# Average pooling by four on one core: input and result buffers resized, all transfers on one queue

## The chip, the cores and the metric

The kernel runs on one core of a Trainium2 chip. The metric is the device time of a whole execution in microseconds. Lower is better. The kernel before takes 1555.81 us, the median of 3 runs from 1555.76 to 1555.83.

## The reference

The input `x` is float32 of shape (64, 256, 8192), the kernel size and the stride are 4. Every group of four neighbours along the last axis becomes its mean:

```python
for i in range(out_len):            # out_len = 2048
    start = i * stride
    output[:, :, i] = np.mean(x[:, :, start : start + kernel_size], axis=2)
```

Because 8192 is a multiple of four and the groups do not overlap, the input can be read as one flat array of 134,217,728 numbers, and the output is a flat array of a quarter of that. 536.87 MB are read and 134.22 MB written.

## The kernel before

The flat array is cut into blocks. A block takes 128 x `w` numbers that lie in one piece in memory; each of the 128 partitions gets `w` of them in a row. There are 63 blocks with `w` = `FULL` = 16384 (64 KB per partition, 8.39 MB), and then a tail of five smaller ones, 8192, 4096, 2048, 1280 and 768 wide. The five tail blocks share one input tile and one result tile, each in a slice of its own.

There are two input buffers of 64 KB per partition (`xin`) and four result buffers of 16 KB (`res`). For each block three functions are called:

- `load` (the DMA is line 62) takes an input buffer and issues the load on SP's queue. Two blocks are loaded ahead; once the first tail block's turn comes, all of the tail is. A load into a buffer that was used before waits, on SP, until the second addition has read that buffer's earlier block.
- `means` adds on VectorE (DVE): line 71 adds even to odd elements in place in the input buffer, line 72 adds the neighbours of that result into the result tile. ScalarE (ACT) multiplies by a quarter in place (line 80). For the last block VectorE does this (line 76).
- `store` (line 85) issues the store of the result. Nearly all stores are issued on ACT's queue; the last full block's and the first tail block's are on SP's.

Each engine executes its instructions in the order in which the program issues them, and waits where an operand or a buffer is not ready. SP's and ACT's DMAs stand in the profile as two queues, q1 and q10. Every DMA between 128 partitions and memory is spread over the core's 16 DMA engines, eight partitions each. In the records of the trace, one partition's row is one packet, and a small packet ends each engine's share of a DMA.

Of the kernel before, what the change touches and what calls it, by code (L numbers as in the profile page):

```python
# [1 line left out]

# [4 lines left out]


FULL = 16384
BUFS_IN = 2  # L10
BUFS_OUT = 4

HEAD = ()
TAIL = (8192, 4096, 2048, 1280, 768)


@with_exitstack
def kernel(
    ctx: ExitStack,
    tc: tile.TileContext,  # L20
    x: bass.AP,
    kernel_size: bass.AP,
    stride: bass.AP,
    out: bass.AP,
):
    nc = tc.nc
    K, S = int(kernel_size), int(stride)
    assert K == S == 4
    B, C, L = x.shape
    assert L % K == 0  # L30
    P = nc.NUM_PARTITIONS
    dt = x.dtype
    add = mybir.AluOpType.add


    xf = x.rearrange("b c l -> (b c l)")
    of = out.rearrange("b c l -> (b c l)")
    rest = B * C * L // P - sum(HEAD) - sum(TAIL)
    assert rest % FULL == 0
    blocks = [(w, i == 0) for i, w in enumerate(HEAD)]  # L40
    blocks += [(FULL, True)] * (rest // FULL)
    blocks += [(w, i == 0) for i, w in enumerate(TAIL)]
    n = len(blocks)
    first = n - len(TAIL)

    pin = ctx.enter_context(tc.tile_pool(name="xin", bufs=BUFS_IN))
    pout = ctx.enter_context(tc.tile_pool(name="res", bufs=BUFS_OUT))

    xs, begins = {}, [0]
    for w, _ in blocks:  # L50
        begins.append(begins[-1] + w)

    def load(i):

        w, fresh = blocks[i]
        if fresh:
            load.tile, load.at = pin.tile([P, FULL], dt, name="xt"), 0
        a = load.at
        load.at += w
        src = xf[P * begins[i] : P * begins[i + 1]].rearrange("(p m) -> p m", p=P)  # L60
        xs[i] = load.tile[:, a : a + w]
        nc.sync.dma_start(out=xs[i], in_=src)  # L62

    def means(i):
        w, fresh = blocks[i]
        if fresh:
            means.tile, means.at = pout.tile([P, FULL // K], dt, name="ot"), 0
        a = means.at
        means.at += w // K
        o, xt = means.tile[:, a : a + w // K], xs.pop(i)  # L70
        nc.vector.tensor_tensor(out=xt[:, : w // 2], in0=xt[:, ::2], in1=xt[:, 1::2], op=add)  # L71
        nc.vector.tensor_tensor(  # L72
            out=o, in0=xt[:, : w // 2 : 2], in1=xt[:, 1 : w // 2 : 2], op=add
        )
        if i == n - 1:
            nc.vector.tensor_scalar(  # L76
                out=o, in0=o, scalar1=1.0 / K, scalar2=None, op0=mybir.AluOpType.mult
            )
        else:
            nc.scalar.mul(o, o, 1.0 / K)  # L80
        return o

    def store(engine, i, o):
        dst = of[P * begins[i] // K : P * begins[i + 1] // K]
        engine.dma_start(out=dst.rearrange("(p m) -> p m", p=P), in_=o)

    loaded = 0
    for i in range(n):

        while loaded < n and (loaded < i + BUFS_IN or loaded > first):  # L90
            load(loaded)
            loaded += 1
        o = means(i)

        store(nc.sync if i in (first - 1, first) else nc.scalar, i, o)


# [1 line left out]
_INS = ['x', 'kernel_size', 'stride']  # L99
_OUTS = [((64, 256, 2048), 'float32')]  # L100

_NUMBERS = {'kernel_size': 4, 'stride': 4}


# [26 lines left out]
```

## Time and profile before

| | |
|---|---|
| median of the runs | 1555.81 us |
| profiled execution, its own time | 1555.85 us |
| its span, first to last instruction | 1554.1 us |
| VectorE busy | 840.5 us (54%) |
| ScalarE busy | 233.1 us (15%) |
| first addition of a full block, 63 times | 8692 ns each |
| second addition of a full block, 63 times | 4426 ns each |
| scaling of a full block, 63 times | 3616 ns each |
| mean DMA rate over the span | 432 GB/s |
| load of a full block, issue to landing | 35.1 us (median) |
| store of a full block on ACT's queue, issue to landing | 31.6 us (median) |

In the profile, DVE is VectorE, ACT is ScalarE, SP is the engine that only issues DMAs here. A name with q behind it (SPq, ACTq) is the engine's instruction queue, where DMAs are issued. `xt` is an input tile and `ot` a result tile. Idle time before an instruction is put down to what ended it, so `[6.17 <-DMA xt<-in_x_dram]` is 6.17 us of waiting that a load's landing ended. In the slices, a digit is the busy share in tenths of one fortieth of the span.

### The profile page before, as it was taken

To read this page: it belongs to the slowest core of one execution; us is meant where nothing else is said; L and a number is where in the kernel's file an instruction comes from. 1 tells how busy PE (TensorE), PEld (TensorE's weight loads), DVE (VectorE), ACT (ScalarE), POOL (GpSimd) and SP (SyncE) were. 2 spreads that over 40 slices of the span, in tenths; PEclk is the share of its full clock that TensorE was granted. 3 is DMA by queue.
4 is the path that set the end of the run, shared out by engine and by line. 5 is a ranking of instruction groups with operands and counts; after the bars stand their busy time and mean duration, and the time that the engine had idled before them with its cause. 6 is when DMAs were issued, how large, how long until landed. Compare 5 with 4: busy or idle time off the path is not lost.

```text
span 1554.1 us, 576 instructions
## 1 busy us (share of the span) xinstructions
DVE 840.5 (54%) x137; ACT 233.1 (15%) x68; POOL 0.2 (0%) x4
## 2 busy tenths in 40 slices
DVE  3646556465464554645546455464554645646557
ACT  1111110110101101011011110111101111011111
POOL 0000000000000000000000000000000000000000
DMA  9999999999999999999999999999999999999999
GB/s 420 416 433 439 439 439 439 427 422 433 439 439 439 436 423 428 434 439 439 437 437 416 434 436 439 439 437 430 420 435 437 439 439 435 431 421 434 438 439 385
DMA packets 19589, 671.14 MB, mean 432 GB/s; under 512 B 2176, under 2 KB 2432, under 8 KB 2944
## 3 DMA queue, kind: packets, MB, share of 16 engines
q1 hardware_dynamic: 10080, 540.02, 80.3%
q10 hardware_dynamic: 9504, 131.08, 19.7%
q14 instruction: 5, 0.04, 0.0%
HBM read 536.87 MB, written 134.22 MB: 432 GB/s over the span
## 4 chain that ended last, share of the span: by engine, by line
DMA 72%; DVE 27%; issue 0%; DVEq 0%; SPq 0%
DMA xt<-in_x_dram 72%; DVE xt L71 18%; DVE ot L72 9%; DVEq L72 0%; SPq L62 0%; DVE ot L76 0%
## 5 line engine op out<-in xcount | busy, mean ns | idle before, releaser
L71 DVE TENSOR_TENSOR xt<-xt 128x8192 f32<-128x8192 f32 (+2 forms) x68 | 556.8, 8190 | 700.5 <-DMA xt<-in_x_dram 700.5
L80 ACT ACTIVATE ot<-ot 128x4096 f32<-128x4096 f32 (+2 forms) x67 | 231.8, 3461 | 1312.8 <-DVE ot L72 1312.8
L72 DVE TENSOR_TENSOR ot<-xt 128x4096 f32<-128x4096 f32 (+2 forms) x68 | 283.8, 4175 | 6.0 <-DVE xt L71 0.5
L80 ACT ACT_TABLE_LOAD x1 | 1.3, 1283 | 0.7 <-PEq L112 0.7
L76 DVE TENSOR_SCALAR ot<-ot 128x192 f32<-128x192 f32 x1 | 0.3, 261 | 0.0
L112 POOL MEMSET const-bfloat16-1.0<- 128x1 bf16 x1 | 0.1, 101 | 0.0
L112 POOL MEMSET const-uint8-127<- 128x1 uint8 x1 | 0.1, 101 | 0.0
L112 POOL MEMSET const-float32-0.0<- 128x1 f32 x1 | 0.1, 98 | 0.2 <-issue 0.2
L112 POOL MEMSET const-float32-1.0<- 128x1 f32 x1 | 0.1, 98 | 0.0
## 6 DMA issues: line engine op xcount, KB each, us to landing
out_dram<-ot ACTq DMA_DIRECT2D x62, 2048.0 KB, 31.6
xt<-in_x_dram SPq DMA_DIRECT2D x1, 4096.0 KB, 25.5
xt<-in_x_dram SPq DMA_DIRECT2D x1, 2048.0 KB, 30.1
out_dram<-ot SPq DMA_DIRECT2D x1, 2048.0 KB, 13.4
xt<-in_x_dram SPq DMA_DIRECT2D x1, 1024.0 KB, 32.1
out_dram<-ot SPq DMA_DIRECT2D x1, 1024.0 KB, 10.5
xt<-in_x_dram SPq DMA_DIRECT2D x63, 35.1
xt<-in_x_dram SPq DMA_DIRECT2D x1, 640.0 KB, 33.8
```

The source lines that it names most:

```text
L71: nc.vector.tensor_tensor(out=xt[:, : w // 2], in0=xt[:, ::2], in1=xt[:, 1::2], op=add)
L72: nc.vector.tensor_tensor(out=o, in0=xt[:, : w // 2 : 2], in1=xt[:, 1 : w // 2 : 2], op=add)
L76: nc.vector.tensor_scalar(out=o, in0=o, scalar1=1.0 / K, scalar2=None, op0=mybir.AluOpType.mult)
L80: nc.scalar.mul(o, o, 1.0 / K)
L112: nc = _bacc.Bacc("TRN2", target_bir_lowering=False, num_devices=1)
```

## The change

The input is cut into groups of `G` = 52,224 numbers per partition. A partition's numbers of one group lie in one piece in memory, so a group is 128 such pieces. A group is loaded by four DMAs, each 13,056 numbers (51 KB) wide per partition: each takes a quarter of every partition's piece. Neighbouring partitions' rows of one load are therefore 208,896 bytes apart in memory. 20 groups make 80 loads; a last load of 4096 numbers per partition takes the rest.

There are three input buffers of 51 KB per partition and one result buffer of 51 KB. The additions and the scaling are the same instructions on narrower tiles. The four tiles of a group write their quarters of the result buffer, and one store of 51 KB per partition writes the group's results, in one piece per partition. In the last group the first three quarters and the last quarter are stored apart. The last load's results are written into its own input buffer and scaled on VectorE.

All DMAs are issued on SP's queue. Three loads are issued at the start. After the instructions of tile `i`, the store (where one is due) is issued and then the load of tile `i + 3`; at that point the loads of tiles `i + 1` and `i + 2` have already been issued. The next group's first write into the result buffer waits for the store of the group before.

```diff
-FULL = 16384
-BUFS_IN = 2
-BUFS_OUT = 4
-TAIL = (8192, 4096, 2048, 1280, 768)
+W = 13056
+LOADS = 4
+BUFS = 3
...
+    G = W * LOADS
+    groups = per // G
+    rest = per - groups * G
+    full = groups * LOADS
...
+    pin = ctx.enter_context(tc.tile_pool(name="xin", bufs=BUFS))
+    pout = ctx.enter_context(tc.tile_pool(name="res", bufs=1))
...
+    def part(flat, a, n):
+        return flat[P * a : P * (a + n)].rearrange("(p m) -> p m", p=P)

     def load(i):
+        g, l = divmod(i, LOADS)
+        xs[i] = pin.tile([P, W], dt, name="xt")
+        if i < full:
+            src = part(xf, g * G, G)[:, l * W : (l + 1) * W]
+            nc.sync.dma_start(out=xs[i][:, :], in_=src)
+        elif i == full:
+            nc.sync.dma_start(out=xs[i][:, :rest], in_=part(xf, groups * G, rest))
...
+    for i in range(BUFS):
+        load(i)
+    for i in range(full):
+        g, l = divmod(i, LOADS)
+        if l == 0:
+            ot = pout.tile([P, G // K], dt, name="ot")
+        o = ot[:, l * W // K : (l + 1) * W // K]
+        sums(xs.pop(i)[:, :], o)
+        nc.scalar.mul(o, o, 1.0 / K)
...
+        cut = (LOADS - 1) * W // K if g == groups - 1 else G // K
+        if (l + 1) * W // K == cut:
+            nc.sync.dma_start(out=part(of, g * G // K, G // K)[:, :cut], in_=ot[:, :cut])
+        elif l == LOADS - 1:
+            nc.sync.dma_start(out=part(of, g * G // K, G // K)[:, cut:], in_=ot[:, cut:])
+        if i + BUFS <= full:
+            load(i + BUFS)
...
+    xt = xs.pop(full)
+    o = xt[:, : rest // K]
+    sums(xt[:, :rest], o)
+    nc.vector.tensor_scalar(out=o, in0=o, scalar1=1.0 / K, scalar2=None, op0=mult)
+    nc.sync.dma_start(out=part(of, groups * G // K, rest // K), in_=o)
```

`sums` holds the two additions that stood in `means`.

More of the change, by code (lines that the diff above doesn't have):

```diff
@@ L6 @@
 from concourse._compat import with_exitstack
-FULL = 16384
-BUFS_IN = 2
-BUFS_OUT = 4
-HEAD = ()
-TAIL = (8192, 4096, 2048, 1280, 768)
+W = 13056
+LOADS = 4
+BUFS = 3
 @with_exitstack
@@ L32, with sums @@
     dt = x.dtype
-    add = mybir.AluOpType.add
+    add, mult = mybir.AluOpType.add, mybir.AluOpType.mult
     xf = x.rearrange("b c l -> (b c l)")
     of = out.rearrange("b c l -> (b c l)")
[L38 to L51, printed above, removed]
-    def load(i):
[L55 to L70, printed above, removed]
+    per = B * C * L // P
+    assert per * P == B * C * L
+    G = W * LOADS
+    groups = per // G
+    rest = per - groups * G
+    assert 0 < rest <= W and rest % (2 * K) == 0
+    full = groups * LOADS
+    pin = ctx.enter_context(tc.tile_pool(name="xin", bufs=BUFS))
+    pout = ctx.enter_context(tc.tile_pool(name="res", bufs=1))
+    xs = {}
+    def part(flat, a, n):
+        return flat[P * a : P * (a + n)].rearrange("(p m) -> p m", p=P)
+    def load(i):
+        g, l = divmod(i, LOADS)
[5 more added lines that the diff above has]
+            nc.sync.dma_start(out=xs[i][:, :rest], in_=part(xf, groups * G, rest))
+    def sums(xt, o):
+        w = xt.shape[1]
         nc.vector.tensor_tensor(out=xt[:, : w // 2], in0=xt[:, ::2], in1=xt[:, 1::2], op=add)
@@ L74, in means @@
         )
[L75 to L95, printed above, removed]
+    for i in range(BUFS):
[19 more added lines that the diff above has]
+    nc.sync.dma_start(out=part(of, groups * G // K, rest // K), in_=o)
 _INS = ['x', 'kernel_size', 'stride']
```

## The prediction

> **What bounds the kernel now.** I read the slices of the span first, then the DMA queues, the chain of waits, the timeline, and last the trace's records of single DMA packets. All lines are of the kernel before.
>
> ```profile
> span 1554.1 us, 576 instructions
> DVE 840.5 (54%) x137; ACT 233.1 (15%) x68; POOL 0.2 (0%) x4
> DMA  9999999999999999999999999999999999999999
> GB/s 420 416 433 439 439 439 439 427 422 433 439 439 439 436 423 428 434 439 439 437 437 416 434 436 439 439 437 430 420 435 437 439 439 435 431 421 434 438 439 385
> ...
> q1 hardware_dynamic: 10080, 540.02, 80.3%
> q10 hardware_dynamic: 9504, 131.08, 19.7%
> ```
>
> The 16 DMA engines are busy in every slice, and the two queues' packets (q1 is SP's, q10 ACT's) fill 100% of the engines' span. VectorE is busy for 54%. The dips in GB/s must not be read as stalls: a slice counts a packet where it starts. The timeline shows that nothing dips:
>
> ```profile
> 42.09 8.69 DVE L71 TENSOR_TENSOR xt<-xt 128x8192 f32<-128x8192 f32 x1 [6.17 <-DMA xt<-in_x_dram]
> ...
> 90.83 8.69 DVE L71 TENSOR_TENSOR xt<-xt 128x8192 f32<-128x8192 f32 x1 [11.04 <-DMA xt<-in_x_dram]
> ...
> 115.01 8.69 DVE L71 TENSOR_TENSOR xt<-xt 128x8192 f32<-128x8192 f32 x1 [11.03 <-DMA xt<-in_x_dram]
> ...
> 139.19 8.69 DVE L71 TENSOR_TENSOR xt<-xt 128x8192 f32<-128x8192 f32 x1 [10.97 <-DMA xt<-in_x_dram]
> ```
>
> Each block starts 24.18 us after the last, here and at 1494.02 and 1518.21. 8.39 MB in and 2.10 MB out in 24.18 us is 434 GB/s.
>
> The chain of waits seems to say that buffers bind, since a load is issued only when the additions free its buffer:
>
> ```profile
> by line: DMA xt<-in_x_dram 72.1%; DVE xt L71 17.9%; DVE ot L72 9.2%; issue 0.2%; DVEq L72 0.1%; SPq L62 0.0%; DVE ot L76 0.0%
> ...
> 104.01 35.16 DMA xt<-in_x_dram
> 139.17 0.02 issue
> 139.19 8.70 DVE xt L71
> ```
>
> But 35.16 us is far more than a load needs: the first two loads land 19.33 us apart (additions at 22.76 and 42.09). The rest is waiting behind the load ahead. The packet records decide it. A 65,536-byte row is one packet and takes 2.418 us in nearly all 8,064 cases, a 16,384-byte one 0.611 us, loads and stores alike; the next packet on an engine starts 4 ns before the last ends, so the pitches are 2.414 and 0.607 us, and the small packet that reports a DMA's end has 6 ns. Eight rows per engine and DMA give 8 x (2.414 + 0.607) + 2 x 0.006 = 24.180 us, the period measured. The kernel runs at the packet rate of the DMA engines, with no gap inside.
>
> **The change, part by part.** *Packets.* Between the two pitches a byte costs (2.414 - 0.607) us / 49,152 = 0.03676 ns, and a packet some 4.7 ns more. A 52,224-byte row is then estimated at 1.9246 us, a DMA of eight rows per engine at 15.403 us. After: 80 loads and 19 stores of that size, 99 x 15.403 = 1524.9; the last load (16,384-byte rows) 4.86; the last group's stores 11.56 and 3.88; the last store 1.25. Sum 1546.45 us. Before: 63 x 24.180 = 1523.34, and 24.53 for the five tail loads and their stores by the same prices: 1547.87. The change saves 1.4 us: 264 packets x 4.7 ns and 33 end packets x 6 ns per engine.
>
> The Trainium skill, page "DMA: Bandwidth & Descriptors", section "Anatomy of one DMA — SWDGE (gpsimd) path", gives a DMA a fixed 2 us or so beside its bytes; for 33 DMAs fewer that would be an estimated 66 us off, which this trace contradicts: a following DMA starts 6 ns later.
>
> *Steady state, buffers.* By the rows of VectorE (8.692 us for 8,192 results, 4.424 for 4,096) the two additions of a 13,056-wide tile take 6.96 and 3.56 us, by ScalarE's (3.616 and 1.911) the scaling 2.92. Let the fourth tile of a group land at 0. It is scaled at 13.9, and SP issues the store, then the next load; SP waits there for ScalarE 3.3 us longer than for the buffer, and only this load is queued behind that wait. Two loads are ahead, until 30.8, so the engines have 17 us of cover. The store runs from 30.8 to 46.2. The next group's first tile landed at 15.4; its second addition must wait for the only result buffer, until about 46.6, some 24 us in all. It ends at 50.2, its buffer's new load is issued, and packets start 1.0 to 2.0 us after an issue (the first load: issued at 0.73, first packets on the engines from 1.73 to 2.74). The load behind the store runs until 61.6. Cover 9.4 us. The next two tiles are finished at 62.1 and 73.8, their loads due at 77 and 92. The fourth lands at 77.0, as the cycle began: VectorE has caught up. So 19 waits of 24 us cost nothing, and the cover does not shrink if a store is slower, since the load behind it moves too.
>
> *Off the path.* The adds come to 80 x 10.52 + 4.5 = 846 us, as now; ScalarE loses 66 DMA issues of 0.34 us, and waits for 1312.8 us anyway. Both lie beside the transfers.
>
> *One queue in place of two.* The trace shows loads after loads on SP's ring, and once stores after loads on it (1541.47: end packet, first store packet 6 ns later), and every change of direction between the two rings, without a gap. It shows no load directly after a store on one ring. Bounds: 0, or at most what a fresh issue costs, 1.0 to 2.0 us x 20 = 20 to 40 us. I take 0, the nearest rows. Nothing is gained below 0, since no gap is there to remove. A store of all engines together, 15.4 us long, is new as well; its nearest row is the end of before, where only stores run from 1541.5 to 1552.8, at 0.611 and 0.309 us a packet as ever.
>
> *Rows with a pitch.* Loads now read 52,224 bytes every 208,896, before they read 8 MB in one piece. No row shows this. Lower bound: the same rate. Upper: the slowest packets of the trace, up to 3.5 us for 2.4 (the first 16, which average 0.68 us over); at 0.68 us x 640 packets 430 us. I take the same rate: each row is one unbroken piece far longer than anything that the records show to suffer.
>
> The page named above, section "Latency and other measured facts", speaks against such pitches: copies with 16 KiB rows lost rate at row pitches of large powers of two (2 MiB: 164 GB/s against 214), and it advises to lay tiles out in one piece. 204 KiB is no power of two, so by it nothing is lost; at the 2 MiB ratio the loads would take an estimated 1.3 times as long. No run here shows either.
>
> *Start and end.* Packets start at 1.73 us in both. Two costs of before may move: 48 packets between 41 and 66 us, when the first store meets the third load, are slow by 0.42 us per engine; I count half as gone, 0.2. And five 8 KB instruction fetches (queue 14) each set one engine back by some 0.55 us; no engine ever makes that up. Most engines are done by 1551.4, the last, hit in the tail, at 1552.85, 1.45 later. The new program is of similar length, so such hits come too; I expect the last engine 0.8 behind, 0.65 less. At the end SP holds the last tile's store until that tile is scaled, 13.9 us after landing; packets by 14.9 to 15.9. The engines have the last load and the three-quarter store until 16.4. That fits by 0.5 us. The last load's additions and scaling, some 4.5 us on VectorE, lie beside the stores.
>
> **Sum.** 1552.85 - 1.4 - 0.2 - 0.65 = 1550.6 for the last packet; from there to the end of the span 1.2 us, as before. Span 1551.8 against 1554.1, so 2.25 us off the profiled execution's own 1555.85, of which 1.75 lie around the span: 1553.6. The median of the runs is 0.04 lower: 1553.5, which is -0.15%, within the 0.2% (3.1 us) that a measurement of this kernel can tell from no change.
>
> **Rivals.** (1) *Faster by over 0.2%.* No engine hit in the tail and all of the 0.42 us gone: 1553.5 - 0.8 - 0.2 = 1552.5, down to 1552.0 with any earlier hits also absent. For it: the fetches sit at places that the program's length sets. Against: five in before. (2) *The ring turns slowly from store to load* or long stores throttle: 20 turns; it needs (1558.9 - 1553.5) / 20 = 0.27 us each to be slower by over 0.2%, at 1.0 us 1573.5. Against it the seamless changes above; for it only that this order was not seen. (3) *Pitched rows read slower.* 640 packets per engine: 8.5 ns each (0.4%) decide, 5% would be 62 us, 1615. (4) *The tail slips.* If the last quarter's addition had to wait for the three-quarter store out of the same tile (landing at 16.8), addition, scaling and issue would put its packets at 24.7 instead of 16.4, some 8.5 us later: 1562. Against: in the tail of before, additions into other slices of a result tile ran at 1541.81 while the store issued at 1535.10 from it was under way or queued:
>
> ```profile
> 1535.10 6.79 SPq L85 DMA_DIRECT2D out_dram<-ot  x2
> ...
> 1541.81 1.23 DVE L72 TENSOR_TENSOR ot<-xt 128x1024 f32<-128x1024 f32 x1
> ```
>
> A mere late issue would cost 0.5 to 2 us: 1554 to 1555.5. (5) *The change does not do as it says:* rows cut into 4 KB packets would add 824 x 12 x 4.7 ns = 46 us. Rows of 768 to 65,536 bytes all went as one packet.
>
> **How the numbers follow.** Forecast, with a late issue: 0.68 (1552.7 to 1555.5). Rival 1: 0.17. Rival 2: 0.05, 3: 0.06, 4 in full: 0.03, 5: 0.01. So faster 0.17, same 0.68, slower 0.15. The range from 1552.2 to 1559.0 leaves out about 0.04 below and 0.14 above; the likeliest case's own is 1552.7 to 1555.5.
>
> **What would show it.** Right: one hardware queue at 100% of the engines, loads of 1.93 us a packet at 434 GB/s; fourths of tiles landing every 77.0 us; VectorE waiting 19 times some 24 us for a store before a group's first second addition; stores landing some 33 us after issue. Wrong: idle slices or lower GB/s once per 77 us (rival 2), longer packets in loads alone (3), a long wait of VectorE in the last 20 us (4). What most likely makes the forecast wrong is a loss in a pattern the trace never showed, pitched loads or a load after a store.

## The result, and the profile after

The changed kernel takes 1558.53 us, the median of 19 runs from 1558.10 to 1559.01; the kernel before takes 1555.83 in the runs beside it. The ratio is 1.0018, with a 95% interval of 1.0011 to 1.0025. So it is 2.7 us slower. That is inside the 0.2% that the prediction called no change, but on the other side of zero than the 2.3 us that it forecast.

The page of the changed kernel, its span, engines, slices and queue:

```profile
span 1556.4 us, 510 instructions
...
DVE 843.5 (54%) x163; ACT 235.1 (15%) x81; POOL 0.2 (0%) x4
...
DMA  9999999999999999999999999999999999999998
GB/s 408 444 415 439 438 432 431 430 436 432 432 435 428 432 436 436 432 432 430 435 435 435 435 430 431 432 439 434 432 431 432 439 434 434 430 431 438 435 434 377
...
q1 hardware_dynamic: 14832, 671.10, 99.8%
```

One queue, a quarter fewer packets, the DMA engines busy everywhere: all of this is as forecast, and none of it shows the loss. "Busy" here means only that a packet is under way on each engine. A packet that takes longer than it needs to also counts as busy, so a page can say 99.8% while microseconds are lost.

The waits of the same kernel (who waited for whom: total us, times, longest):

```profile
DVE xt L64 <- DMA xt<-in_x_dram: 539.7, 80, 19.1
DVE ot L65 <- DMA out_dram<-ot: 163.1, 19, 8.7
```

The single result buffer makes VectorE wait 19 times, as forecast, but for 8.6 us, not 24: the second addition is held up just as long, from the end of the first at 87.77 to 112.55 below, but meanwhile VectorE does the next tile's first addition (96.97). The prediction had taken the order of the kernel's text for the order on VectorE; they are not the same here.

The first loss is visible in the timeline, in the starts of the first additions (start us, duration, engine, line). Only loads are under way until the load that lands last here; the first store, issued at 78.91, stands in the queue behind it:

```profile
49.94 6.96 DVE L64 TENSOR_TENSOR xt<-xt 128x6528 f32<-128x6528 f32 x1 [4.88 <-DMA xt<-in_x_dram]
...
65.37 6.96 DVE L64 TENSOR_TENSOR xt<-xt 128x6528 f32<-128x6528 f32 x1 [4.88 <-DMA xt<-in_x_dram]
...
78.91 0.35 SPq L81 DMA_DIRECT2D out_dram<-ot  x1
...
80.81 6.96 DVE L64 TENSOR_TENSOR xt<-xt 128x6528 f32<-128x6528 f32 x1 [4.89 <-DMA xt<-in_x_dram]
...
96.97 6.96 DVE L64 TENSOR_TENSOR xt<-xt 128x6528 f32<-128x6528 f32 x1 [9.20 <-DMA xt<-in_x_dram]
112.55 7.03 DVE L65 TENSOR_TENSOR ot<-xt 128x3264 f32<-128x3264 f32 x2 [8.62 <-DMA out_dram<-ot]
```

Tiles land 15.43 and 15.44 us apart, then one lands after 16.16 us. That load stands ahead of the store in the queue, so the store's bytes are not yet in it. The packet records say where the 0.7 us are: the last of each engine's eight load packets, the one right before the first store packet, took 2.29 to 3.11 us in place of 1.928, on all 16 engines.

Call the most frequent time of a size's packets its price, and a packet "late" that is over it by more than 0.04 us. Then the records give these sums for the kernels below (us per engine, a sixteenth of the total; the first 16 packets, 0.63 to 0.81 in every kernel, are left out):

| kernel | late, 12 to 154 us | late, after 154 us | all smaller excess |
|---|---|---|---|
| before | 0.44 | 0.12 | 0.11 |
| before, a shorter tail | 0.19 | 0.12 | 0.13 |
| changed kernel | 0.83 | 1.16 | 1.50 |
| changed, VectorE's order at the end | 0.75 | 0.87 | 1.70 |
| changed, group stores on ACT's queue | 0.20 | 1.08 | 1.40 |
| changed, loads in one piece | 1.02 | 0.71 | 1.62 |
| changed, a store per tile, SP | 2.24 | 0.44 | 0.22 |
| changed, a store per tile, ACT's queue | 0.35 | 0.12 | 0.15 |
| changed, engines set apart first | 3.98, before the first store | 0.43 | 1.97 |
| before, stores on SP | 1.70 | 1.02 | 0.18 |
| before, a store per two blocks | 1.01 | 13.56 | 0.22 |

In the kernel before, what is late after 154 us are the packets beside instruction fetches. Each row is one trace. The changed kernel and those with loads in one piece or another order at the end issue their stores alike, so their rows show how far such sums vary by themselves: 0.75 to 1.02 and 0.71 to 1.16. The two rows of before with the same first blocks have 0.44 and 0.19.

### The profile page after: what moved, and what is told of

Its sections match the earlier page's. It is cut to its first block, busy times and chain, and to the rows that moved or that the text cites. A ratio compares the mean times of both kernels' runs of the same rounds, so it can differ in the third digit from the quotient of the medians.

```text
span 1556.4 us, 510 instructions
## 1 busy us (share of the span) xinstructions
DVE 843.5 (54%) x163; ACT 235.1 (15%) x81; POOL 0.2 (0%) x4
## 3 DMA queue, kind: packets, MB, share of 16 engines
q1 hardware_dynamic: 14832, 671.10, 99.8%
## 4 chain that ended last, share of the span: by engine, by line
DMA 77%; DVE 19%; ACT 4%; issue 0%; DVEq 0%
DMA out_dram<-ot 40%; DMA xt<-in_x_dram 37%; DVE xt L64 10%; DVE ot L65 9%; ACT ot L77 4%; DVEq L65 0%
## 5 line engine op out<-in xcount | busy, mean ns | idle before, releaser
L64 DVE TENSOR_TENSOR xt<-xt 128x6528 f32<-128x6528 f32 (+1 forms) x81 | 558.9, 6900 | 539.7 <-DMA xt<-in_x_dram 539.7
L77 ACT ACTIVATE ot<-ot 128x3264 f32<-128x3264 f32 x80 | 233.8, 2922 | 1313.1 <-DVE ot L65 1313.1
L65 DVE TENSOR_TENSOR ot<-xt 128x3264 f32<-128x3264 f32 x80 | 282.9, 3556 | 164.6 <-DMA out_dram<-ot 163.1
## 6 DMA issues: line engine op xcount, KB each, us to landing
out_dram<-ot SPq DMA_DIRECT2D x19, 6528.0 KB, 32.8
```

What stands on the lines that cost most here:

```text
L65: nc.vector.tensor_tensor(out=o, in0=xt[:, : w // 2 : 2], in1=xt[:, 1 : w // 2 : 2], op=add)
```

## The experiments

Two theories went in. One (called T in the first three expectations, S in the later ones): whenever the engines begin to store after a stretch of loads alone, load packets in flight are drawn out, unevenly. The other (P): rows 208,896 bytes apart are slow to load. More came up on the way.

**Stores on a queue of their own.**

```diff
-            nc.sync.dma_start(out=part(of, g * G // K, G // K)[:, :cut], in_=ot[:, :cut])
+            q = nc.sync if g == groups - 1 else nc.scalar
+            q.dma_start(out=part(of, g * G // K, G // K)[:, :cut], in_=ot[:, :cut])
```

> The 19 group stores go on ScalarE's queue, the last group's and the rest as in the changed kernel. Changed kernel: 1558.5 us. Theory T (turn): what the changed kernel loses is lost where all engines turn together from loads to a long store on one ring; the last load packet before the first store was 0.83 us late on every engine, before later stores 0.04 to 0.26 us on average and up to 0.85 us on single engines, some 2.1 us in all for the engine that ends last. With a second ring store and load packets alternate, so this goes: 1555.5 to 1556.2; the lag between first and last engine stays near 1 us in place of 3.2. Rival P (pitch): loads of rows 208,896 bytes apart are slower, the ring does not matter: 1558.2 to 1558.9.

Measured: a median of 1560.06 us over ten runs, ratio 1.0036 (1.0019 to 1.0052), with runs anywhere from 1558.53 to 1599.92; eight of them lie below 1569, with a median of 1559.55. Both expectations missed. The first start was cheaper (0.20 us), but all later ones cost as much as on one queue (1.08 against 1.16). A second queue by itself is not the cure. In this kernel too the store queue is empty most of the time and starts anew for every group.

**Loads in one piece.**

```diff
-            src = part(xf, g * G, G)[:, l * W : (l + 1) * W]
+            src = part(xf, i * W, W)
```

> Every load reads 6.68 MB in one piece (row pitch 52,224 bytes) in place of rows 208,896 bytes apart; the stores are those of the changed kernel, so each result goes to another place than the reference has it. Rival P: the 20 to 35 ns that the second, third and fourth load after a store take over the packet price (1.6 us in all) go, and perhaps the slow packets ahead of the stores too: 1555 to 1557. Theory T: nothing changes but chance hits, 1558.0 to 1559.0.

Measured: 1558.31 us (1558.08 to 1559.01), the changed kernel's time. The late packets and the smaller excess stay (1.02, 0.71 and 1.62), and the load ahead of the first store again lands late:

```profile
80.88 6.96 DVE L64 TENSOR_TENSOR xt<-xt 128x6528 f32<-128x6528 f32 x1 [4.89 <-DMA xt<-in_x_dram]
97.40 6.96 DVE L64 TENSOR_TENSOR xt<-xt 128x6528 f32<-128x6528 f32 x1 [9.56 <-DMA xt<-in_x_dram]
```

The pitch of the rows costs nothing here, and theory P falls. The Trainium skill, page "DMA: Bandwidth & Descriptors", section "Latency and other measured facts", warns of pitches of large powers of two; this pitch is none, and the run agrees that it is harmless.

**A store for each tile, on SP's queue.**

```diff
-    pout = ctx.enter_context(tc.tile_pool(name="res", bufs=1))
+    pout = ctx.enter_context(tc.tile_pool(name="res", bufs=LOADS))
...
+        ot = pout.tile([P, W // K], dt, name="ot")
+        o = ot[:, :]
...
+        at = l * W // K
+        nc.sync.dma_start(out=part(of, g * G // K, G // K)[:, at : at + W // K], in_=o)
```

> All on SP's queue, but a store of 13,056 bytes per row for each tile (80 stores, four result buffers of a quarter). By packets and ends alone 2.5 us more than the changed kernel. Theory T with a cost per turn of the ring (0.1 us on average): 60 turns more cost 6 us and more: 1564 to 1570. Theory T with a cost that hangs on the length of the store's packets: the losses at turns go (2.5 us) and so do those of loads that follow loads (1.6 us), since each load now follows a store: 1556.5 to 1557.5. Rival P: 1560.5 to 1561.5.

Measured: 1564.20 us (1561.90, the profiled run, to 1565.17). The time is what the theory with a cost for each turn said, but the records say something else. The late packets are nearly all in the first dozen stores:

```profile
90.27 6.96 DVE L64 TENSOR_TENSOR xt<-xt 128x6528 f32<-128x6528 f32 x1 [9.39 <-DMA xt<-in_x_dram]
...
109.99 6.96 DVE L64 TENSOR_TENSOR xt<-xt 128x6528 f32<-128x6528 f32 x1 [9.11 <-DMA xt<-in_x_dram]
...
129.82 6.96 DVE L64 TENSOR_TENSOR xt<-xt 128x6528 f32<-128x6528 f32 x1 [9.22 <-DMA xt<-in_x_dram]
...
1018.10 6.96 DVE L64 TENSOR_TENSOR xt<-xt 128x6528 f32<-128x6528 f32 x1 [8.66 <-DMA xt<-in_x_dram]
...
1037.38 6.96 DVE L64 TENSOR_TENSOR xt<-xt 128x6528 f32<-128x6528 f32 x1 [8.68 <-DMA xt<-in_x_dram]
```

19.72 and 19.83 us a tile early on, 19.28 later; by packets it is 8 x (1.9246 + 0.4847) + 0.012 = 19.286. The spread between the first and the last engine to end a DMA grows meanwhile from 0.7 to 2.6 us, and then stays between 2.5 and 2.9. So here starts cost while the engines are close together, and drive them apart. The rest of the time went at the end, where only 8.7 us of transfers cover the last tile's additions and scaling; that wait also hides part of the lateness, so this kernel's time by itself decides nothing.

**VectorE's order at the end.**

```diff
-    sums(xt[:, :rest], o)
+    with tc.issue_after(last[1].ins):   # last[1]: the last full tile's second addition
+        sums(xt[:, :rest], o)
```

> Only the order of VectorE at the end is changed: the last full tile's second addition goes ahead of the last small tile's first. The last quarter's store is issued 2.2 us earlier, and the engine that ends last no longer idles before it (0.45 us): 1557.9 to 1558.2. Rival: the end is set by that engine's lag alone and by the smaller stores: 1558.4 to 1558.7.

Measured: 1557.86 us (1557.56 to 1558.15), 0.67 less than the changed kernel. First the changed kernel's end, then this one's:

```profile
1533.32 9.16 DVE L64 TENSOR_TENSOR xt<-xt 128x6528 f32<-128x6528 f32 x2 [4.89 <-DMA xt<-in_x_dram]
1542.39 3.55 DVE L65 TENSOR_TENSOR ot<-xt 128x3264 f32<-128x3264 f32 x1
...
1548.93 0.34 SPq L83 DMA_DIRECT2D out_dram<-ot  x1
```

```profile
1532.88 6.96 DVE L64 TENSOR_TENSOR xt<-xt 128x6528 f32<-128x6528 f32 x1 [4.87 <-DMA xt<-in_x_dram]
1539.87 3.56 DVE L67 TENSOR_TENSOR ot<-xt 128x3264 f32<-128x3264 f32 x1
1543.35 2.28 DVE L64 TENSOR_TENSOR xt<-xt 128x2048 f32<-128x2048 f32 x1
...
1546.41 0.34 SPq L86 DMA_DIRECT2D out_dram<-ot  x1
```

In the changed kernel two first additions (x2, 9.16 us) run before the second addition that the last store needs. That store is issued 15.6 us after its tile's work begins, here 13.5.

**No group stores.**

```diff
-        if (l + 1) * W // K == cut:
+        if (l + 1) * W // K == cut and g == groups - 1:
...
-        elif l == LOADS - 1:
+        elif l == LOADS - 1 and g == groups - 1:
```

> The 19 stores of groups 0 to 18 are left out (124 MB of the output are not written); loads, additions and the end are those of the changed kernel. By packets 19 x 15.403 = 292.7 us less: 1265.8. Theory S (starts of storing): each time the engines, after a stretch of loads alone, begin to store, the load packets in flight are drawn out, unevenly, which drives the engines apart; once they are 2.5 to 3 us apart it costs little. Without stores no load packet is late between 80 us and the end (in the changed kernel 1.9 us per engine), the engines stay about 1 us apart in place of 3.2, and a load takes less than 10 ns over its packets (20 to 35 in the changed kernel): 1261 to 1263. Rival L: loads that follow loads are slow by themselves: 20 to 35 ns per load stay, 1264 to 1265.

Measured in one run: 1264.19 us. No packet is late after the first ones but beside instruction fetches, and the engines stay within 0.7 us of each other until such a fetch; so lateness comes with the stores. But rival L was right as well. From the seventh load on every load takes some 30 ns over the price, with no store near:

```profile
698.62 6.96 DVE L64 TENSOR_TENSOR xt<-xt 128x6528 f32<-128x6528 f32 x1 [4.88 <-DMA xt<-in_x_dram]
...
714.07 6.96 DVE L64 TENSOR_TENSOR xt<-xt 128x6528 f32<-128x6528 f32 x1 [4.82 <-DMA xt<-in_x_dram]
...
729.51 6.96 DVE L64 TENSOR_TENSOR xt<-xt 128x6528 f32<-128x6528 f32 x1 [4.90 <-DMA xt<-in_x_dram]
```

15.45 and 15.44 us, where packets make 15.40. In the changed kernel the first load after a store takes its price, and the next three some 15 to 30 ns more. Without the group stores the last engine, put back by an instruction fetch, ends its loads 0.8 us behind the mean of all.

**Engines set apart before the first store.**

```diff
+    early = pout.tile([P, G // K], dt, name="ot")   # the first group's result buffer
+    load(0)
+    row = 0
+    for n in range(14, 0, -2):
+        nc.sync.dma_start(out=early[row : row + n, :2880], in_=part(xf, 0, W)[:n, :2880])
+        row += n
+    for i in range(1, BUFS):
+        load(i)
...
```

> The changed kernel with seven small loads more behind the first one, of 14, 12, ... 2 rows of 11,520 bytes, into the result buffer before it is used (their data are never read). If a DMA of n rows goes on the n lowest engines, a pair of engines is 0.43 us behind the next one, 3.0 us from first to last. Theory S: with the engines apart from the start, the load packets ahead of the first store are late by less than 0.3 us on average (0.83 in the changed kernel), ahead of all later stores by less than 0.5 us together (1.1); the last engine ends about where it did: 1558 to 1559.5. Rival N (every start costs what it costs, first touch or number): the late packets stay and the 3 us come on top: 1560.5 to 1562.

Measured: 1563.96 us (1563.50 to 1564.66), outside both ranges. The time is off, since the small loads disturbed each other and the load beside them: 52 of their 56 packets took 0.47 to 1.6 us in place of 0.43. But they did set the engines 2.66 us apart, and around the first store not one packet was late. In the changed kernel all 16 engines' were. The load ahead of the store (it lands at 103.98 here) takes no longer than another, 15.43 us:

```profile
88.55 6.96 DVE L64 TENSOR_TENSOR xt<-xt 128x6528 f32<-128x6528 f32 x1 [4.89 <-DMA xt<-in_x_dram]
103.98 6.96 DVE L64 TENSOR_TENSOR xt<-xt 128x6528 f32<-128x6528 f32 x1 [8.47 <-DMA xt<-in_x_dram]
```

Later starts together cost 0.43 us, below the 0.71 to 1.16 of the three kernels that store alike. That is theory S's answer, and rival N's falls. But the distance is not all: in the changed kernel the second start cost 0.04 us with the engines 1.1 us apart, hardly more than the 0.9 at the first, which cost 0.83; and the fifth and sixth, with the engines 1.5 to 2.1 us apart, cost 0.14 and 0.27. What else sets the cost of a start is not shown.

**A store for two blocks, in the kernel before.** (The results go to other places of the output than the reference has them.)

```diff
-BUFS_OUT = 4
+BUFS_OUT = 2
...
+        if i < first - 1:
+            if i % 2:
+                dst = of[P * begins[i - 1] // K : P * begins[i + 1] // K]
+                nc.scalar.dma_start(out=dst.rearrange("(p m) -> p m", p=P), in_=means.tile[:, :])
+            continue
```

> The kernel before, with one thing changed: the full blocks' results are stored two blocks at a time (32 KB per row, on ScalarE's queue, two result buffers of 32 KB). So the store queue empties between stores and storing starts 31 times, while before it starts once and then always goes on. Theory S: load packets are late at the starts, mostly in the first dozen, and the engines end up 2.5 us or more apart where they were 1.0: 1557 to 1558.5. Rival by packet count: 248 packets per engine fewer, -1.2 us: 1554.6 to 1555.

Measured: four runs of 1554.89, 1570.28, 1580.82 and 1585.33 us. One run has the time that packets alone give, the others lose 15 to 30 us. In the profiled one (1570.28) late packets cost 1.1 us in the first 600 us, and then they came at start after start, 13.6 us in all, with the engines up to 3.6 us apart and 5 at the end. So stopping and starting again does cost, but "mostly in the first dozen" is wrong for two queues, and being apart does not protect this kernel. What sets the cost of a start there stays open.

**All stores on SP's queue, in the kernel before.**

```diff
-        store(nc.sync if i in (first - 1, first) else nc.scalar, i, o)
+        store(nc.sync if i <= first else nc.scalar, i, o)
```

> The kernel before with all full blocks' stores on SP's queue in place of ScalarE's, nothing else. Each store of 4.9 us then stands between two loads of 19.3 us, and storing starts 63 times. Theory S: 2 to 3 us lost in the first dozen or two: 1557.5 to 1559. Rival (one queue costs nothing, as the prediction had it): 1555.5 to 1556.1.

Measured: 1558.69 us (nine of ten runs from 1557.97 to 1559.16, one 1578.61), ratio 1.003 (1.0005 to 1.0056). One part of the change done alone, with the packets of before, costs as much as the whole change. That the two sizes agree is chance: here storing starts 63 times and late packets make 2.7 us, while the changed kernel loses 2.0 us in late packets and 1.5 in smaller excess. First additions again:

```profile
67.15 8.69 DVE L71 TENSOR_TENSOR xt<-xt 128x8192 f32<-128x8192 f32 x1 [11.99 <-DMA xt<-in_x_dram]
91.67 8.69 DVE L71 TENSOR_TENSOR xt<-xt 128x8192 f32<-128x8192 f32 x1 [11.36 <-DMA xt<-in_x_dram]
116.16 8.69 DVE L71 TENSOR_TENSOR xt<-xt 128x8192 f32<-128x8192 f32 x1 [11.35 <-DMA xt<-in_x_dram]
141.10 8.69 DVE L71 TENSOR_TENSOR xt<-xt 128x8192 f32<-128x8192 f32 x1 [11.72 <-DMA xt<-in_x_dram]
```

24.52, 24.49 and 24.94 us a block, where two queues have 24.19, 24.18 and 24.18 in the same place. The Trainium skill, page "DMA: Bandwidth & Descriptors", section "Issuing engines are not separate DMA queues", holds that transfers from several engines share the same DMA engines and that a second issuing engine saves only time on the sequencer. Here that second queue is worth 2.8 us, and the DMA engines never stand idle for an issue before the tail; the measurement decides.

**A store for each tile, on ACT's queue.** As the third experiment, with `nc.scalar.dma_start`, and with the order at the end of the fourth.

> As the kernel with one 13,056-byte-row store per tile, but with these stores on ScalarE's queue (and the last small tile's additions behind the last full tile's). A store then goes packet by packet beside a load, 19.3 us long, and the next is issued before it is done, so storing starts once and never stops. Theory S: after the first 100 us the late load packets sum to less than 0.2 us per engine and fetch (0.8 us and more in the kernels where storing starts again and again), the engines stay within 1.2 us, and loads have no 30 ns over their packets. By packets 2.5 us over the changed kernel's, and the last store finds some 6 us of idle engines, since only one store and the small load cover the last scaling: 1560.5 to 1562.5. Rival N: each store start costs, on whichever queue: late packets as with the stores on SP's queue, and 1563 to 1566.

Measured: 1562.70 us (1562.67 to 1562.74), 0.2 above theory S's range and below rival N's. First additions:

```profile
91.91 6.96 DVE L64 TENSOR_TENSOR xt<-xt 128x6528 f32<-128x6528 f32 x1 [8.73 <-DMA xt<-in_x_dram]
...
111.23 6.96 DVE L64 TENSOR_TENSOR xt<-xt 128x6528 f32<-128x6528 f32 x1 [8.70 <-DMA xt<-in_x_dram]
...
130.50 6.96 DVE L64 TENSOR_TENSOR xt<-xt 128x6528 f32<-128x6528 f32 x1 [8.66 <-DMA xt<-in_x_dram]
```

19.32 and 19.27 us where the same stores on SP's queue gave 19.72 and 19.83 at the same place. Between 77 and 385 us no packet is over its price at all. The engines stay 0.56 us apart until instruction fetches hit them, and are 1.9 apart at the end. Storing never stops here: each store runs beside a whole load, and the next is issued before it is done, just as in the kernel before. The kernel is slow for another reason: its last store is issued at 1553.39, 14 us after its tile's first addition began at 1539.79, with little left to transfer meanwhile: the engines stand idle for 5.7 to 7.5 us before it.

**A shorter tail, in the kernel before.** `TAIL = (8192, 4096, 4096)`.

> The kernel before with the tail cut into 8192, 4096 and 4096 in place of five pieces; a try at a faster kernel. Two loads and two stores fewer: 0.15 us of packets. In the kernel before two instruction fetches set engines back in the tail, and the last engine ended 1.45 us behind most others; if a shorter program moves these, up to 1.4 us: 1554.3 to 1555.7. If the tail's length in VectorE counts, it is slower: 1556 to 1557.

Measured: 1555.76 us (1555.49 to 1556.18), ratio 1.0 (0.999 to 1.0009). The two late instruction fetches came at 1535.15 and 1541.01 as before; nothing is won. No kernel of these that writes the whole output in its place beats the kernel before.

## Why the prediction was wrong

*What bounds the kernel* was right, and so was the price of packets: 264 fewer per engine at 4.7 ns, and a DMA of 52,224-byte rows at 15.403 us; the records have 15.403 or 15.404 wherever nothing disturbs it. The 1.4 us of gain are in the packets. (The page that the prediction cites for 2 us a DMA gives them for DMAs issued by GpSimd, and none here is; the 6 ns between DMAs in a queue rest on the trace alone.)

*Buffers* were right: no idle DMA engine in the middle, stores landing 32.8 us after issue (33 were forecast), groups 77.1 us apart (77.0). Only VectorE's order beside the wait for the result buffer was wrong, and that cost nothing in the middle.

*One queue in place of two* is the step that failed. It took 0 for the turns, from rows that did not carry it: the change from loads to stores that it cited, at 1541.47, was one in the tail, after load packets of 3 KB. The cost is at the change from loads to stores, not the other way round as rival 2 had it, and it sits in the load packet ahead of the store, so that no gap ever shows. Rival 2 looked at the turns of the queue, though at the other one, and put the point of decision at 0.27 us a turn; measured are about 0.1 us, (0.83 + 1.16) / 20. The trace of before did show the effect once, the 48 slow packets from 41 us on. The prediction saw them, tied them to "the first store meets the third load", and booked them as a cost that might shrink. They were the cost of a start of storing, which the kernel before pays once.

The sum put the last packet at 1550.6; it ended at 1555.17. The difference of 4.6 us, by the records and runs:

- the first start: 0.2 forecast, 0.83 measured, so 0.6;
- later starts: 0 forecast, 1.16 measured, of which 0.1 beside instruction fetches as before, so 1.0;
- loads after loads: 0 forecast, 1.50 of smaller excess measured (0.11 before), so 1.4 (15 to 30 ns for each of some 60 loads);
- the last engine: 0.8 behind the mean forecast, 1.9 measured when it is done with the three-quarter store, so 1.1;
- VectorE's order at the end: the last engine then stands idle for 0.45 until the last quarter's store is issued. The estimate of that issue, 13.9 us after landing, had no other instruction between the two additions. The run that mends the order gains 0.67 in the median.

These come to 4.6. The run without group stores has no late packets but beside fetches, and its last engine is 0.8 behind, so the first, second and fourth come with the stores; the fifth has a run of its own. The same run shows that loads after loads are 0.2% slow with no store near; why, no run shows.

*Pitched rows* (rival 3): right to take none; the run with loads in one piece shows it. *The tail slips* (rival 4): it did, by another way than the one priced and for less (0.45 us). *Rows as single packets* (rival 5): as forecast.

## What to carry to other kernels

Where DMA engines are busy throughout, look at the length of packets, not at gaps: time is lost inside packets that still count as busy, and the spacing of landings shows it. In these kernels stores cost only their packets, after the first, as long as storing never stopped, with one store per load on a second queue and the next issued before the last was done; one queue, or stores gathered into fewer and larger ones, gave back more than the saved packets were worth. A slow spell that a trace shows once, at a first time, has to be looked at for every time that the change makes it happen again.

## What the runs showed of the hardware

- When all 16 engines went from loads to their first store within about 1 us, the last load packet of each took up to 1.2 us more (changed kernel, 93 us). With the engines 2.66 us apart, none did. The second start cost 0.04 us with the engines 1.1 us apart, so the distance is not all. Whether the memory or the engines hold the packets up, no run here tells.
- Where loads follow loads in a queue, the packets of the second to fourth load took some 2 to 4 ns more than those of the first load after a store (1.930 to 1.932 against 1.928 us), except in the first 100 (no group stores) to 200 us (changed kernel). The packets of a load that follows a store had 1.928 us though seven of the eight stand behind another load packet (a store per tile on SP's queue), so it is not the packet just ahead that matters.
- An 8 KB instruction fetch put one DMA engine back by some 0.5 to 1.0 us, and the engine stayed behind for the rest of the kernel.
- Two kernels that issue stores on the second queue with pauses between them had times that varied by 10 us and more from run to run (1558.5 to 1568.5 in eight of ten; 1554.9 and 1570.3 in two of four); the kernels whose stores never pause varied by at most 1.2 (before, 1555.68 to 1556.88). Of the ten runs with all stores of before on SP's queue one took 20 us more than the rest. What makes these runs long is not shown.
